# Feed-forwards of a hybrid encoder trunk as seven block products instead of eight, with the weight sums on GpSimd

## The chip, the cores and the metric

The kernel runs on one core of a Trainium2 chip. The core's engines work side by side, each with its own queue of instructions: TensorE (PE in the rows; its weight loads are PEld), VectorE (DVE), ScalarE (ACT), GpSimd (POOL), and SyncE (SP), which here only starts transfers. The metric is the device time of one execution in microseconds (us).

## What is computed

Two layers over 512 tokens of 1024 features, all in float32. Each layer has two SwiGLU feed-forwards with 2816 inner features, so there are four feed-forwards in a run; between them stand a mixer (layer 0: sliding-window attention beside a gated recurrence; layer 1: a gated delta rule), layer normalisations and a gated embedding. Cut to what matters here:

```
def swiglu(x, wg, wu, wd):
    return (jax.nn.silu(x @ wg) * (x @ wu)) @ wd

for i in range(2):
    x = layer_norm(DN_ALPHA * x + 0.5 * swiglu(x, ffn1_wg[i], ffn1_wu[i], ffn1_wd[i]), ...)
    y = mixer_ab(x, ...) if i % 2 == 0 else mixer_c(x, ...)
    x = layer_norm(DN_ALPHA * x + y, ...)
    x = layer_norm(DN_ALPHA * x + 0.5 * swiglu(x, ffn2_wg[i], ffn2_wu[i], ffn2_wd[i]), ...)
    x = x + sigmoid(x @ ple_wg[i] + ple_bg[i]) * (p[i] @ ple_wp[i])
```

## The kernel before

Activations lie with features on the 128 partitions and the 512 tokens along the free axis, so x is eight tiles `xf[k]` of 128x512, and the inner features of a feed-forward are 22 tiles `hs[j]`. Weights come as tiles of 128x128, packed by the host in the order of use: one transfer on SyncE's queue brings eight of them (512 KB, tile name `wr`), into one of three buffers.

A float32 product is carried by three float32r matmuls (`mm3`). Both operands are cut into a rounded part `hi` and the remainder `lo = src - hi`: ScalarE makes `hi` (the rows' CAST), VectorE subtracts (TENSOR_TENSOR with two inputs). The weights are cut four tiles at a time, 128x512 per instruction, by the generator `splitter`, which runs some steps (`self.ahead`; a step is one product of a block in the changed kernel, where `AHEADS` sets it) in front of the products; activations are cut by `split` when they are made.

`ffn` makes the gate and up products of two inner tiles at a time (`group`: four PSUM banks advance together over the eight k), and `evac` turns them into `hs[j]` with a Silu on ScalarE and a product on VectorE. Then `resid_ln` makes the down products, one output tile of 22 k at a time (`mtile`), adds them to the residual and takes sums for the layer normalisation; the two adds of sums per output tile are the only large work of GpSimd (`add.l.tensor_tensor` with `G`). The last output tile is made by halves of the tokens, so that `tail` and `apply` normalise the first half under the products of the second.

Tile by tile that is 3 x 8 x 22 = 528 weight tiles for a feed-forward, 1584 matmuls, of 512 columns except for those of the last output tile (and of the first group, where a layer normalisation stands in front of it), which go by 256.

The order of issue is made at build time. The main stream is TensorE's; everything else is a generator that yields operations, and `tick` lets each go on as far as its operands are there by a rough clock of every engine (`Eng.cost`). Each engine then works through its own queue in that fixed order. Nearly every instruction is issued from one line, `getattr(self.e, op.name)(*op.a, **op.kw)` in `Eng.issue`, which is L100 in the rows of before (L151 in the order of the changed kernel); so rows are told apart by tile names: `wr` raw weights, `t` any 128x512 tile of the pool, `ps` a PSUM bank.

Of the kernel before, what the change touches and what calls it, by code (L numbers as in the profile page):

```python
# [35 lines left out]
NRAW = 3  # L36
NTILES = 4 * 3 * KD * MF + 2 * (KD + 2) * KD + (14 + 8) * KD + 8 + (32 + 8) * KD
NUNITS = -(-NTILES // NSLOT)
# [4 lines left out]
# columns of the packed per-partition vectors  # L43
# [14 lines left out]
# columns of the constant table: identity, ones, cumulative-sum triangle, causal mask,  # L58
# compact identity, masks of the block-doubling levels
# [16 lines left out]
def cells(ap):  # L76
    """the 128-element columns of its tile that an access touches"""
    name = ap.tensor.name
    dims = list(ap.ap)
    c0 = ap.offset % dims[0][0]  # L80
    c1 = c0 + sum((n - 1) * st for st, n in dims[1:])
    return [(name, c) for c in range(c0 // P, c1 // P + 1)]


class Eng:
    """Issues to an engine and keeps a rough clock of it, by which the order of issue of
    independent work is chosen. eng.f(...) issues, eng.l.f(...) makes an Op to be issued later."""
# [25 lines left out]
    def at(self, op):  # L113
        """when the operands are there"""
        ready = self.k.ready
        return max([ready.get(c, 0.0) for x in op.ins for c in cells(x)] + [0.0])

    def cost(self, op):
# [7 lines left out]
        if self.kind == "PE":  # L126
            if op.name == "transpose":
                return max(0.027, 0.000417 * w)
            if ins[0].dtype == F32R:
                return max(0.107, 0.000417 * w) + 0.0025  # L130
            return 2 * max(0.107 * n / P, 0.000417 * w) + 0.004
# [18 lines left out]
        return 0.04 + (0.0008 if op.name == "memset" else 0.0023) * n  # L150
# [10 lines left out]
class Kern:  # L161
    def __init__(self, tc, a, order):
# [5 lines left out]
        self.nslot = 0  # L168
        self.units, self.raw = {}, {}
        self.ndma = self.nsplit = 0  # L170
# [62 lines left out]
    def tick(self, share=None):  # L233
        """share: the time that chains may take on the tensor engine now"""
# [39 lines left out]
    def until(self, cond):  # L274
        """hold the main stream until the chains have issued what it needs"""
# [8 lines left out]
    def settle(self, *aps):  # L284
        """chains go on while the main stream's next operands are not there"""
# [7 lines left out]
    def dma_unit(self, v):  # L293
        t = self.wraw.tile([P, NSLOT * P], F32, tag="wraw", name=self.name("wr"))
        self.nc.sync.dma_start(t, self.a["w"][v])
        self.raw[v] = t
        self.landing(t, 3.5)

    def splitter(self):
        """splits the weights some half units ahead of their use"""  # L300
        while self.nsplit < 2 * NUNITS:
            v = self.nsplit
            while v > self.nslot // HSLOT + self.ahead:
                yield None
            while self.ndma <= min(v // 2 + NRAW - 1, NUNITS - 1):
                self.dma_unit(self.ndma)
                self.ndma += 1
            r = self.raw[v // 2] if v % 2 == 0 else self.raw.pop(v // 2)
            r = r[:, (v % 2) * HSLOT * P:(v % 2 + 1) * HSLOT * P]
            hi, lo = self.tl(), self.tl()  # L310
            for c0, c1 in FIRST if v == 0 else ((0, HSLOT),):
                if c1 <= HSLOT:
                    c = slice(c0 * P, c1 * P)
                    yield self.S.l.copy(hi[:, c].bitcast(F32R), r[:, c])
                    yield self.V.l.tensor_tensor(lo[:, c].bitcast(F32R), r[:, c], hi[:, c], ALU.subtract)
                    self.units[v] = (hi, lo)
            self.nsplit += 1

    def w(self, desc):
        """the next weight tile of the stream, as its two parts"""  # L320
        u, s = divmod(self.nslot, HSLOT)
        if s == 0:
            # the splitter goes first when it is late
            late = self.nsplit <= u + 2
            prio = 0 if late else 4
            if prio != self.split_gen[2] and self.split_gen in self.gens:
                self.gens.remove(self.split_gen)
                self.split_gen[2] = prio
                self.enlist(self.split_gen)
            self.until(lambda: u in self.units)  # L330
            self.units.pop(u - 1, None)
        self.order.append(desc)
        self.nslot += 1
        hi, lo = self.units[u]
        s = slice(s * P, (s + 1) * P)
# [19 lines left out]
    def split(self, src, eng=None):  # L355
        """hi = rounded src, lo = src - hi; src in SBUF or PSUM"""
# [8 lines left out]
    def group(self, descs, x, nk=KD, halves=False):  # L365
        """the m tiles of a group advance together over k; with halves, tokens 0-255 first"""
# [20 lines left out]
    def x(self, k, cs):  # L387
        """layer input k, once its normalisation is issued"""
# [12 lines left out]
    def ffn(self, i, n, l):  # L401
        wg, wu, wd = f"ffn{n}_wg", f"ffn{n}_wu", f"ffn{n}_wd"
        self.hs = [None] * MF
        self.ahead = 4

        def evac(j, pg, pu):
            t = self.tl()
            yield self.S.l.activation(t, pg, AF.Silu)
            self.psfree(self.S)
            yield self.V.l.tensor_tensor(t, t, pu, ALU.mult)  # L410
            self.psfree(self.V)
            self.hs[j] = yield from self.split(t)

        for g in range(MF // 2):
            descs = []
            for j in (2 * g, 2 * g + 1):
                descs.append(lambda k, j=j: (wg, i, k, j))
                descs.append(lambda k, j=j: (wu, i, k, j))
            ps = self.group(descs, self.x, halves=g == 0 and n == 2)
            for j in range(2):  # L420
                self.spawn(evac(2 * g + j, ps[2 * j], ps[2 * j + 1]), 1)
        self.resid_ln(i, l, 0.5, lambda m: (lambda k: (wd, i, k, m)), self.h, MF, 0, 1)

    def resid_ln(self, i, l, fac, desc, y, nk, ngroup, nhalf):
        """x = LN(alpha x + fac y); y comes as 8 PSUM tiles: the first ngroup advance together
        over k, the last nhalf are made by halves of the tokens, so that the normalisation of the
        first half runs under the products of the second. Sums are taken about the mean of the
        first 128 features."""
        S, V, G, PE = self.S, self.V, self.G, self.PE
        self.__dict__.pop("x", None)  # L430
        xf = self.xf
# [39 lines left out]
        for m in range(max(ngroup, 1), KD - nhalf):  # L471
            if m == KD - nhalf - 2 or nk == KD:
                self.ahead = AHEADF if nk == MF else AHEADO
# [80 lines left out]
    def ple_p(self, i, ms):  # L554
        """products of p, made where the main stream would wait for a normalisation"""
# [13 lines left out]
    def ple(self, i):  # L569
# [26 lines left out]
        if last:  # L596
            # the last one by halves of the tokens, each on its way out under the other
# [17 lines left out]
        self.x = x  # L615

    def softplus(self, x, n):
        """max(x,0) + log1p(exp(-|x|)), log1p by 2 atanh(e/(2+e))"""
# [74 lines left out]
    def attn(self, j, hh, q):  # L693
        """one head, two pairs of 128-query blocks; keys of the block and of the one before"""
# [59 lines left out]
    def conv(self, p_, cols, bias=None):  # L754
        """causal depthwise convolution over the free axis, taps w[0..3] per partition"""
# [142 lines left out]
    def gdn(self, h):  # L898
# [9 lines left out]
        # decay: dt[j, i] = exp(gc_i - gc_j), j <= i  # L908
# [3 lines left out]
        # token-major k, q (for the norms) and v  # L912
# [37 lines left out]
        # U = (I + N)^-1, 32x32 diagonal blocks first (compact), then 64 and 128  # L950
# [15 lines left out]
        # level s: with the 2s blocks [lo | hi], the product of U11 N12 with U22 makes U12; two  # L966
        # chunks share a pass, the hi (then the lo) columns of both being 32
# [52 lines left out]
        # scan over the blocks  # L1020
# [48 lines left out]
    def run(self):  # L1069
# [3 lines left out]
        with ExitStack() as es:  # L1073
# [12 lines left out]
            r0 = self.wraw.tile([P, NSLOT * P], F32, tag="wraw", name="wr0")  # L1086
            self.raw[0] = r0
            self.ndma = 1
# [209 lines left out]
```

## Time and profile before

| | us |
|---|---|
| three runs | 2113.21, 2113.46 (median), 2114.86 |
| span of the profiled execution | 2113.2 |
| PE busy | 2093.3 (99%) |
| DVE busy | 1102.8 (52%) |
| ACT busy | 867.1 (41%) |
| POOL busy | 145.5 (7%) |

The profiled execution has no time of its own beside its span; the span lies 0.3 us under the median. Times below are in us from the span's start. A duration in a row runs from an instruction's start to its end and holds its waits once it has been dispatched; instructions of one engine overlap a little, so the pace of a run of equal ones is the length of the run, less the overhang of the last, by their number.

### The profile page before, as it was taken

The page shows a single profiled execution, that of the slowest core. Times are in us where ns is not written, and L with a number is a line of the kernel's source. Part 1 is how long each engine was busy: PE and PEld are TensorE (multiplying, and loading weights), DVE is VectorE, ACT ScalarE, POOL GpSimd, SP SyncE. Part 2 cuts the span into 40 slices and gives each one's busy share as a digit, 9 for nine tenths or more (in the row PEclk, how much of TensorE's full clock was granted, in tenths as well). Part 3 has the DMA queues.
Part 4 walks back from the last instruction along what each step waited for, and adds up shares of the span by engine and source line. Part 5 has one row for each costly group of instructions (what it writes and reads, how often), then busy time and mean ns, then how long its engine had stood idle before and what let it go on. Part 6 is the DMA issues. An engine that isn't in the chain of part 4 may idle for free. (4 is left out here: it accounts for less than half of the span.)

```text
span 2113.2 us, 29415 instructions
## 1 busy us (share of the span) xinstructions
PE 2093.3 (99%) x11773; PEld 1757.3 (83%) x11773; DVE 1102.8 (52%) x2146; ACT 867.1 (41%) x1795; POOL 145.5 (7%) x120
## 2 busy tenths in 40 slices
PE   9999999999999999999999999999999999999999
PEld 7888888878888888898888888977777898888888
DVE  5334345778833334484333344867776763343456
ACT  4323224665623322263323223674754452232244
POOL 0000012001100001100000011020210200000110
PEclk9999999999999999999999999999999999999999
DMA  5323234113232323313232324132221213232331
GB/s 180 118 81 105 85 110 150 41 52 99 79 102 81 119 80 101 133 56 110 90 109 80 110 87 143 33 85 65 51 63 59 90 62 119 80 113 78 108 120 51
DMA packets 55754, 194.38 MB, mean 92 GB/s; under 512 B 6320, under 2 KB 7232, under 8 KB 55616
## 3 DMA queue, kind: packets, MB, share of 16 engines
q1 hardware_dynamic: 54432, 188.81, 27.6%
q0 software_dynamic: 1184, 3.69, 0.9%
q8 instruction: 92, 1.51, 0.3%
q14 instruction: 46, 0.38, 0.1%
HBM read 190.35 MB, written 2.11 MB: 91 GB/s over the span
## 5 line engine op out<-in xcount | busy, mean ns | idle before, releaser
L100 PE MATMUL ps<-t,t 128*128 128x512 f32 (+5 forms) x10640 | 2049.8, 354 | 7.1 <-ACT t L100 4.3
L100 PEld LDWEIGHTS ps<-t,t 128*128 128x128 f32 (+3 forms) x10640 | 1692.4, 184 | 319.2 <-issue 17.8
L100 DVE TENSOR_TENSOR t<-wr,t 128x512 fp32r<-128x512 f32 (+1 forms) x695 | 485.7, 741 | 163.7 <-ACT t L100 159.3
L100 ACT CAST t<-wr 128x512 fp32r<-128x512 f32 (+1 forms) x695 | 393.8, 616 | 193.2 <-DMA wr<-w 192.9
L100 DVE TENSOR_TENSOR t<-t,ps 128x512 f32<-128x512 f32 (+1 forms) x126 | 71.1, 565 | 440.3 <-PE ps L100 251.9
L100 ACT ACTIVATE t<-ps 128x512 f32<-128x512 f32 (+2 forms) x172 | 78.9, 462 | 501.6 <-PE ps L100 501.3
L100 DVE TENSOR_TENSOR t<-t,t 128x512 fp32r<-128x512 f32 (+3 forms) x314 | 176.0, 571 | 62.6 <-ACT t L100 56.1
L100 POOL TENSOR_TENSOR t<-t,t 128x512 f32<-128x512 f32 x64 | 98.3, 1555 | 1601.8 <-DVE t L100 1581.9
L100 ACT CAST t<-t 128x512 fp32r<-128x512 f32 (+1 forms) x253 | 130.0, 518 | 162.7 <-DVE t L100 160.0
L100 ACT ACTIVATE t<-t 128x512 f32<-128x512 f32 (+1 forms) x118 | 66.4, 572 | 260.6 <-DVE t L100 256.6
L100 DVE SCALAR_TENSOR_TENSOR t<-ps,t 128x512 f32<-128x512 f32 (+2 forms) x74 | 43.9, 600 | 212.5 <-PE ps L100 212.5
L100 DVE SCALAR_TENSOR_TENSOR t<-ps,vec,t 128x511 f32<-128x511 f32 (+3 forms) x92 | 68.2, 743 | 21.1 <-ACT t L100 17.4
L100 ACT ACTIVATE t<-t,vec,der 128x256 f32<-128x256 f32 x96 | 55.2, 597 | 5.8 <-DVE t L100 5.8
L100 ACT ACT_TABLE_LOAD x37 | 47.5, 1283 | 10.7 <-DVE t L100 9.5
L100 DVE SCALAR_TENSOR_TENSOR t<-t,t 128x512 f32<-128x512 f32 (+2 forms) x64 | 38.2, 605 | 21.0 <-ACT t L100 19.7
L100 DVE SCALAR_TENSOR_TENSOR t<-t,der,t 128x256 f32<-128x256 f32 x96 | 45.8, 477 | 0.0
L100 ACT COPY t<-ps 128x512 f32<-128x512 f32 (+1 forms) x59 | 33.0, 567 | 28.1 <-PE ps L100 27.9
L100 PEld LDWEIGHTS ps<-cst,t 128*128 128x128 f32 (+1 forms) x300 | 35.4, 148 | 10.8 <-issue 2.3
L100 PE MATMUL ps<-cst,t 128*128 128x128 f32 (+2 forms) x300 | 41.5, 261 | 1.4 <-DVE t L100 1.4
L100 DVE TENSOR_TENSOR t<-t 128x256 f32<-128x256 f32 x96 | 40.1, 420 | 2.6
L100 POOL TENSOR_TENSOR y<-y,sm 128x8 f32<-128x8 f32 (+1 forms) x16 | 22.9, 1434 | 190.0 <-DVE y L100 189.9
L100 ACT ACTIVATE t<-ps,vec 128x512 f32<-128x512 f32 x28 | 19.4, 699 | 23.8 <-PE ps L100 23.8
(66 smaller groups left out, 412.8 us busy)
## 6 DMA issues: line engine op xcount, KB each, us to landing
wr<-w SPq DMA_DIRECT2D x346, 512.0 KB, 4.2
t<-x SPq DMA_DIRECT2D x8, 256.0 KB, 6.3
t<-p SPq DMA_DIRECT2D x8, 256.0 KB, 5.0
t<-gcd POOLq DMA_DIRECT2D x8, 256.0 KB, 5.3
out<-t SPq DMA_DIRECT2D x7, 256.0 KB, 2.0
t<-bias POOLq DMA_DIRECT2D x8, 192.0 KB, 3.7
cst<-cst SPq DMA_DIRECT2D x1, 352.0 KB, 5.8
wr<-w SPq DMA_DIRECT2D x2, 128.0 KB, 2.9
```

Source lines behind the costliest of these rows:

```text
L100: getattr(self.e, op.name)(*op.a, **op.kw)
```

## The change

In most of a feed-forward two k tiles, two output tiles and the two halves of the tokens now form a 2x2 by 2x2 block product, made by seven products of 256 columns instead of eight (the scheme of Winograd). `block` makes one such block over `n` pairs of k tiles: seven products (`PRODUCTS`), each 3n matmuls of 256 columns; three of them go into the PSUM bank R one after the other, and between them ScalarE takes a copy of R (`snap`), for which the next product into R waits. The five sums that the seven weight forms need are made of raw weights by `adder` on GpSimd (four instructions a block); the seven forms are then cut into hi and lo by `splitter`. The forms of the activations (four differences and seven or eight splits for a pair of tiles, all of 256 columns) are made by `xforms` for x and by `hforms` for the inner features. `gate_up(j)` is a block whose two output tiles are gate and up of inner tile j; `down(mp, ...)` one whose output tiles are 2mp and 2mp+1.

The 22 inner tiles are taken in three parts of 6, 8 and 8; after each part its share of the down products is added to the residual. Two of the inner tiles (`NPLAIN`), and the last two output tiles in the third part, are still made by plain products. Per feed-forward there are 20 blocks of `gate_up` with 4 pairs, 4 of `down` with 3 pairs, and 4 + 3 of `down` with 4 pairs. Raw buffers go from 3 to 5, pool tiles from 93 to 89; the rough clock has new costs for matmuls and GpSimd. Mixers and embeddings keep their code.

The diff, cut to its core:

```diff
-NRAW = 3
+NRAW = 5
+PARTS = (6, 8, 8)
+NPLAIN = 2
+PRODUCTS = ("a11", "a12", "s2", "s3", "s1", "a22", "s4")
+AHEADS, SUMAHEAD = 4, 3
...
+    def adder(self):
+        G = self.G.l
+        for it, (v, u, n) in enumerate(self.st.items):
...
+            a11, a12, a21, a22 = r0[:, 0:n], r0[:, n:2 * n], r1[:, 0:n], r1[:, n:2 * n]
+            s1, s2, s3, s4 = (self.tl() for _ in range(4))
...
+            yield G.tensor_tensor(s1[:, 0:n], a21, a22, ALU.add)
...
+            yield G.tensor_tensor(s2[:, 0:n], s1[:, 0:n], a11, ALU.subtract)
...
+            yield G.tensor_tensor(s3[:, 0:n], a11, a21, ALU.subtract)
...
+            yield G.tensor_tensor(s4[:, 0:n], a12, s2[:, 0:n], ALU.subtract)
...
+    def block(self, descs, forms, pairs, done):
...
+        def snap(name, p_):
+            yield S.activation(snaps[name], p_[:, TA], AF.Copy, scale=scale)
...
+        product(R, "a11", True, True)
+        self.spawn(snap("s1", R), 0)
+        X = self.ps()
+        product(X, "a12", True, True)
+        self.spawn(done("c11", X, snaps["s1"], lambda: "s1" in have), 1)
+        wait("s1")
+        product(R, "s2", False, True)
+        self.spawn(snap("s2", R), 0)
+        Q = self.ps()
+        product(Q, "s3", True, True)
+        self.spawn(snap("q1", Q), 0)
+        wait("s2")
+        product(R, "s1", False, True)
+        self.spawn(snap("s4", R), 0)
+        wait("q1")
+        product(Q, "a22", False, True)
+        self.spawn(done("c21", Q, snaps["s2"], lambda: True), 1)
+        self.spawn(done("c22", snaps["q1"], snaps["s4"], lambda: "s4" in have), 1)
+        wait("s4")
+        product(R, "s4", False, True)
+        self.spawn(done("c12", R, None, lambda: True), 1)
...
+    def diffs(self, b0, b1, F, key, home=None, free=None):
...
+            yield V.tensor_tensor(d, x, y, ALU.subtract)
...
+            yield from self.halves_split(d, hi, lo)
...
+        def gate_up(j):
...
+                if name == "c11":
+                    yield V.tensor_tensor(g[:, cs], p_[:, TA], s, ALU.add)
+                    self.psfree(self.V)
+                    yield S.activation(g[:, cs], g[:, cs], AF.Silu)
+                elif name == "c12":
+                    yield S.activation(g[:, cs], p_[:, TA], AF.Silu)
+                    self.psfree(self.S)
+                elif name == "c21":
+                    yield V.tensor_tensor(u[:, cs], p_[:, TA], s, ALU.add)
+                    self.psfree(self.V)
+                else:
+                    yield G.tensor_tensor(u[:, cs], p_, s, ALU.add)
...
+                if n[half] == 2:
+                    yield V.tensor_tensor(h[:, cs], g[:, cs], u[:, cs], ALU.mult)
...
+        def down(mp, pairs, end):
...
+                if s is not None:
+                    yield V.tensor_tensor(x, x, s, ALU.add)
+                if name == "c22":
+                    yield V.tensor_tensor(x, x, p_, ALU.add)
+                else:
+                    yield V.scalar_tensor_tensor(x, p_[:, TA], 0.5, x, ALU.mult, ALU.add)
```

How the queues move is seen at two places. First VectorE in the middle of the first feed-forward's gate and up products. Before, weights are cut one after the other, and now and then an inner tile (`t_660`, `t_667`) is made and cut:

```order
L100 TENSOR_TENSOR t_632<-wr_545,t_631 128x512
L100 TENSOR_TENSOR t_650<-wr_579,t_649 128x512
L100 TENSOR_TENSOR t_660<-t_660,ps_502 128x512
L100 TENSOR_TENSOR t_664<-t_660,t_663 128x512
L100 TENSOR_TENSOR t_667<-t_667,ps_504 128x512
L100 TENSOR_TENSOR t_672<-t_667,t_671 128x512
L100 TENSOR_TENSOR t_684<-wr_579,t_683 128x512
L100 TENSOR_TENSOR t_702<-wr_613,t_701 128x512
```

In the changed program, at one block of `gate_up` (its c11 and c21 read the banks `ps_2355` and `ps_2394`; `t_2434` and `t_2452` are cut from sums, the 256-wide rows are products and forms of inner tiles):

```order
L151 TENSOR_TENSOR t_2325<-ps_2355,t_2327 128x256
L151 TENSOR_TENSOR t_2379<-t_2169,t_2378 128x512
L151 TENSOR_TENSOR t_2398<-wr_2058,t_2397 128x512
L151 TENSOR_TENSOR t_2415<-wr_2058,t_2414 128x512
L151 TENSOR_TENSOR t_2434<-t_2332,t_2433 128x512
L151 TENSOR_TENSOR t_2326<-ps_2394,t_2327 128x256
L151 TENSOR_TENSOR t_2325<-t_2325,t_2326 128x256
L151 TENSOR_TENSOR t_2452<-t_2333,t_2451 128x512
L151 TENSOR_TENSOR t_2457<-t_2325,t_2456 128x256
L151 TENSOR_TENSOR t_2325<-t_2325,t_2326 128x256
L151 TENSOR_TENSOR t_2485<-t_2160 128x256
L151 TENSOR_TENSOR t_2492<-t_2331,t_2491 128x512
```

What moved: cuts of weight forms now come seven to a block, and small instructions with two tile inputs stand between them. Second, GpSimd, which before has nothing in its queue between the start and the adds of the first layer normalisation:

```order
L100 MEMSET sm 128x8
L100 ISA
L100 TENSOR_TENSOR t_2023<-t_80,t_81 128x512
L100 TENSOR_TENSOR t_2022<-t_2022,t_2112 128x512
L100 TENSOR_TENSOR t_2023<-t_2023,t_82 128x512
```

In the changed program the same queue, in the gate and up products of the first feed-forward, holds the four sums of each block (inputs `wr`), and after the sums of the next block the c22 of an earlier one (`t_1558`):

```order
L151 TENSOR_TENSOR t_1455<-wr_1286 128x512
L151 TENSOR_TENSOR t_1456<-t_1455,wr_1241 128x512
L151 TENSOR_TENSOR t_1457<-wr_1241,wr_1286 128x512
L151 TENSOR_TENSOR t_1458<-wr_1241,t_1456 128x512
L151 TENSOR_TENSOR t_1578<-wr_1405 128x512
L151 TENSOR_TENSOR t_1579<-t_1578,wr_1358 128x512
L151 TENSOR_TENSOR t_1580<-wr_1358,wr_1405 128x512
L151 TENSOR_TENSOR t_1581<-wr_1358,t_1579 128x512
L151 TENSOR_TENSOR t_1558<-t_1560 128x256
```

What moved: GpSimd goes from two adds per output tile at the end of a feed-forward to work in every block, all of it with inputs in SBUF.

## Rows read from the trace of the kernel before

**Rows 1.** Page: busy time of the engines and waits of all TensorE matmuls.
```profile
PE 2093.3 (99%) x11773; PEld 1757.3 (83%) x11773; DVE 1102.8 (52%) x2146; ACT 867.1 (41%) x1795; POOL 145.5 (7%) x120
L100 PE MATMUL ps<-t,t 128*128 128x512 f32 (+5 forms) x10640 | 2049.8, 354 | 7.1 <-ACT t L100 4.3
```

**Rows 2.** Windows inside the four feed-forwards: busy us, instructions, granted clock, DMA share, GB/s.
```profile
core 0: us, PE busy (x) PEld busy (x) DVE busy (x) ACT busy (x) POOL busy (x), PEclk, DMA share, GB/s
20.00:340.00 320.00, 320.00 (x1413) 264.97 (x1412) 127.39 (x212) 100.24 (x181) 15.12 (x10) 1.00 0.32 104
...
570.00:880.00 310.00, 310.00 (x1387) 257.42 (x1387) 118.70 (x179) 94.98 (x170) 12.30 (x8) 1.00 0.31 100
960.00:1290.00 330.00, 330.00 (x1457) 273.27 (x1456) 125.90 (x191) 100.81 (x180) 12.30 (x8) 1.00 0.31 101
...
1720.00:2040.00 320.00, 320.00 (x1414) 264.96 (x1413) 121.68 (x182) 96.14 (x173) 15.31 (x10) 1.00 0.33 105
```

**Rows 3.** Timeline, PE: unbroken runs of 512 and of 256 columns (start, length).
```profile
149.81 113.95 PE L100 MATMUL ps<-t,t 128*128 128x512 f32 x502
...
923.74 16.48 PE L100 MATMUL ps<-t,t 128*128 128x256 f32 x136
```

**Rows 4.** Timeline, DVE and ACT: runs of equal instructions, back to back, GpSimd idle.
```profile
30.57 3.09 DVE L100 TENSOR_TENSOR t<-wr,t 128x512 fp32r<-128x512 f32 x5
...
368.99 1.42 DVE L100 TENSOR_TENSOR t<-t,t 128x256 f32<-128x256 f32 x4
...
248.04 2.71 ACT L100 CAST t<-wr 128x512 fp32r<-128x512 f32 x5
```

**Rows 5.** Timeline, DVE and POOL, around 324: layer normalisation adds beside weight cuts.
```profile
322.23 3.31 POOL L100 TENSOR_TENSOR t<-t,t 128x512 f32<-128x512 f32 x2 [11.95 <-DVE t L100]
...
322.00 5.89 DVE L100 TENSOR_TENSOR t<-wr,t 128x512 fp32r<-128x512 f32 x6
...
323.80 1.74 POOL L100 TENSOR_TENSOR t<-t,t 128x512 f32<-128x512 f32 x1
324.31 1.77 DVE L100 TENSOR_TENSOR t<-wr,t 128x512 fp32r<-128x512 f32 x1
```

**Rows 6.** Timeline, the same two engines around 527: a 256-column DVE instruction.
```profile
525.94 1.75 POOL L100 TENSOR_TENSOR t<-t,t 128x512 f32<-128x512 f32 x1
526.45 1.52 DVE L100 TENSOR_TENSOR t<-t,t 128x256 f32<-128x256 f32 x1
```

**Rows 7.** Timeline around 523: POOL beside DVE instructions with one PSUM input.
```profile
521.72 2.55 POOL L100 TENSOR_TENSOR t<-t,t 128x512 f32<-128x512 f32 x2 [155.99 <-DVE t L100]
522.67 0.67 DVE L100 SCALAR_TENSOR_TENSOR t<-ps,t 128x512 f32<-128x512 f32 x1
...
528.49 0.41 DVE L100 SCALAR_TENSOR_TENSOR t<-ps,t 128x256 f32<-128x256 f32 x1
528.83 1.18 DVE L100 TENSOR_TENSOR t<-t,t 128x256 f32<-128x256 f32 x1
```

**Rows 8.** Groups, by form: scaling of x on DVE, and evacuations on ACT.
```profile
L100 DVE TENSOR_SCALAR t<-t 128x512 f32<-128x512 f32 x14 | 5.9, 418 | 0.3 <-ACT t L100 0.2
L100 ACT ACTIVATE t<-ps 128x256 f32<-128x256 f32 x12 | 4.5, 377 | 3.5 <-PE ps L100 3.5
```

**Rows 9.** Page: issues of the weight transfers (count, KB each, us to landing).
```profile
wr<-w SPq DMA_DIRECT2D x346, 512.0 KB, 4.2
```

More of the change, by code (lines that the diff above doesn't have):

```diff
@@ L312, in splitter @@
                 if c1 <= HSLOT:
[L313 to L317, printed above, removed]
-    def w(self, desc):
[L321 to L332, printed above, removed]
+                    c = slice(c0 * P, min(c1 * P, n))
@@ L402, in ffn, with xforms @@
         wg, wu, wd = f"ffn{n}_wg", f"ffn{n}_wu", f"ffn{n}_wd"
-        self.hs = [None] * MF
+        S, V, G = self.S.l, self.V.l, self.G.l
         self.ahead = 4
+        xdone, xs, xf = self.xdone, self.xs, self.xf
+        XF = {}
+        last = len(PARTS) - 1
+        hf, HF, HP = {}, {}, {}
+        scaled = []
+        def xforms(kp):
+            k0, k1 = 2 * kp, 2 * kp + 1
+            while not (xdone(k0) and xdone(k1)):
+                yield None
+            for which, k, cs in (("a11", k0, TA), ("a12", k1, TA), ("s4", k1, TB)):
+                XF[kp, which] = tuple(t[:, cs] for t in xs(k))
+            yield from self.diffs(xf[k0], xf[k1], XF, kp, tuple(t[:, TB] for t in xs(k0)),
+                                  lambda: self.nplain == NPLAIN)
+            for m in (k0, k1):
+                yield V.tensor_scalar(xf[m], xf[m], ALPHA, None, ALU.mult)
+            scaled.append(kp)
@@ L406, in evac @@
         def evac(j, pg, pu):
             t = self.tl()
-            yield self.S.l.activation(t, pg, AF.Silu)
+            yield S.activation(t, pg, AF.Silu)
             self.psfree(self.S)
-            yield self.V.l.tensor_tensor(t, t, pu, ALU.mult)
+            yield V.tensor_tensor(t, t, pu, ALU.mult)
             self.psfree(self.V)
[L412 to L421, printed above, removed]
@@ new lines, in down, with done @@
+        def down(mp, pairs, end):
+            ends = {}
+            def done(name, p_, s, ready):
+                m, cs = 2 * mp + int(name[1]) - 1, TA if name[2] == "1" else TB
+                x = xf[m][:, cs]
+                while not ready() or len(scaled) < KD // 2:
+                    yield None
+                if s is not None:
+                    yield V.tensor_tensor(x, x, s, ALU.add)
+                if name == "c22":
+                    yield V.tensor_tensor(x, x, p_, ALU.add)
+                else:
+                    yield V.scalar_tensor_tensor(x, p_[:, TA], 0.5, x, ALU.mult, ALU.add)
+                    self.psfree(self.V)
+                ends[m] = ends.get(m, 0) + 1
+                if ends[m] == 2:
+                    end(m)
+            self.snapscale = 0.5
+            self.block((lambda k: (wd, i, k, 2 * mp), lambda k: (wd, i, k, 2 * mp + 1)),
+                       lambda kp, r: HF.get((kp, r)), pairs, done)
+            self.snapscale = 1.0
@@ new lines, in ffn @@
+        self.nplain = 0
+        for kp in range(KD // 2):
+            self.spawn(xforms(kp), 2.5)
+        descs = []
+        for j in range(NPLAIN):
+            descs.append(lambda k, j=j: (wg, i, k, j))
+            descs.append(lambda k, j=j: (wu, i, k, j))
+        ps = self.group(descs, self.x, halves=n == 2)
+        for j in range(NPLAIN):
+            self.spawn(evac(j, ps[2 * j], ps[2 * j + 1]), 1)
+        self.nplain = NPLAIN
+        j1 = 0
+        for n_, part in enumerate(PARTS):
+            j0, j1 = j1, j1 + part
+            self.ahead = AHEADS
+            for j in range(j0, j1):
+                if j % 2 == 0:
+                    self.spawn(hforms(j // 2, n_ == last), 1.2)
+                if j >= NPLAIN:
+                    gate_up(j)
+            pairs = range(j0 // 2, j1 // 2)
+            if n_ < last:
+                for mp in range(KD // 2):
+                    down(mp, pairs, lambda m: None)
@@ L471, in resid_ln @@
         for m in range(max(ngroup, 1), KD - nhalf):
-            if m == KD - nhalf - 2 or nk == KD:
-                self.ahead = AHEADF if nk == MF else AHEADO
+            self.ahead = AHEADO
             self.spawn(take(m, self.mtile(desc(m), y, nk), FULL, True, G), 1)
@@ L615, in ple @@
         self.x = x
+        self.xdone = self.xs = lambda k: new[k]
     def softplus(self, x, n):
```

326 lines of the change are left out of this document (290 added, 36 removed).

## Prediction

> **What bounds the kernel now.** I read the page first, then windows inside the four feed-forwards, then single stretches of the timeline. The page says that TensorE is busy for 2093.3 of the 2113.2 us, and that its 10640 main matmuls were preceded by 7.1 us of idle time in all [rows 1]. In four windows that lie inside the feed-forwards it never pauses, at the full granted clock (1.00, the 2.4 GHz level), while VectorE is busy 38 to 40%, ScalarE 31% and GpSimd 4 to 5% [rows 2]. So the count and the pace of matmuls set the time there, and everything else has room.
>
> The pace: 502 matmuls of 512 columns took 113.95 us, 0.227 us each; 136 of 256 columns took 16.48, of which some 0.16 is the last one's overhang, so 0.120 each [rows 3]. Half the columns cost 53%, not 50%: each matmul carries about 13 ns that do not shrink.
>
> **TensorE's share of the change.** A feed-forward before has 528 tiles x 3 = 1584 matmuls; without the last output tile that is 1518 of 512 columns (344.6 us) and 132 of 256 (15.8): 360.4 us. After: the blocks hold 20x4 + 4x3 + 7x4 = 120 pairs, each 7 x 3 matmuls of 256 columns, 2520 in all; the plain rest is 32 tiles of gate and up (96 of 512 columns) and 16 of down by halves (96 of 256). That is 21.8 + 2616 x 0.120 = 335.7 us. Four feed-forwards save 4 x 24.7 = 99 us; a pace of 0.121 for the narrow ones would make it 89. The first group that goes by halves is the same in both.
>
> The Trainium skill ("TensorE: Matmul & The Clock Gate", Back-to-back issue gap) gives 518 cycles for 512 columns and 262 for 256, a fixed cost of some 2.5 ns. By it 5688 fewer wide and 9936 more narrow ones would save 142 us, by the rows 99; the rows decide.
>
> **What VectorE and GpSimd must do instead.** The question is whether they can feed TensorE at that pace. Alone, VectorE cuts 512 columns every 0.602 us (five in 3.09, less 0.08 overhang) and does a 256-column instruction with two tile inputs every 0.335 (four in 1.42) [rows 4]. But when GpSimd works, the two take turns. Six cuts took 5.89 us with two GpSimd adds among them, instead of 6 x 0.602 + 0.08 = 3.69: 1.10 us lost per add [rows 5]. In detail: the add ends at 325.54, the cut dispatched at 324.31 ends at 326.08, 0.54 later, its whole working time behind the add [rows 5]; a 256-column one ends at 527.97, 0.28 behind the add that ended at 527.69 [rows 6]. An instruction with one input in PSUM is not held: two adds in 2.55 us while such ones went by at 0.67 [rows 7]. So each GpSimd sum of 512 columns stops the VectorE instructions with two SBUF inputs for about 1.1 us. The changed kernel has four such sums per block, and nearly all that it adds on VectorE has two SBUF inputs.
>
> The Trainium skill says this as a rule ("SBUF — State Buffer", Who interferes with whom): the pair of ports is locked for whole instructions, and VectorE instructions with two SBUF inputs contend with GpSimd ones that read SBUF. The rows agree (1.10 us of loss against none), and the rule speaks against this change: it says that the sums are not free on an idle engine.
>
> Now the stages, for one feed-forward, as VectorE's own line of time:
> - *Two blocks of gate_up* (two inner tiles): 14 cuts (8.43), 15 instructions of 256 columns with two SBUF inputs (4 products of gate and up, 11 for the forms of the pair; 5.03), 4 adds from PSUM (0.34 by the step from 528.49 to 528.83 [rows 7], 1.36): 14.8. GpSimd: 8 sums x 1.10 and two c22 of 256 columns, which no row shows. I bound these by half and the whole of 1.10 and take half, being half the columns: 9.9. Together 24.7; the four adds from PSUM can lie under GpSimd work, so 23.4 to 24.7, and I take 24.2. TensorE needs 168 x 0.120 = 20.2; before it was 96 x 0.227 = 21.8. So +2.4, times ten: **+24**, bounds +16 and +29.
> - *A down block of four pairs*: 7 cuts (4.21), 4 adds with two SBUF inputs (1.34), 3 with PSUM (1.02), 4 sums (4.4): 11.0, less at most 1.02; TensorE 10.1; before 10.9. I take 10.5. Four in the second part: **-1.6** (-3.3 to +0.4).
> - *A down block of three pairs*: cuts and sums of 384 columns at three quarters (no row; between half and whole): 3.2 + 1.3 + 1.0 + 3.3 = 8.8, less at most 1.0; TensorE 7.6; before 8.2. I take 8.5. Four: **+1.3** (-0.8 to +2.6).
> - *Start*: 32 forms of x (10.7), 8 scalings (3.4 at 0.42 [rows 8]), 12 cuts (7.2), 4 sums (4.4), some evacuation (1.9): 27.6 beside 21.8 of plain products. Only the third product of the first block needs differences, so I take **+2** (0 to +5.8).
> - *Last part's down* (three blocks, then 16 plain tiles): TensorE 30.2 + 11.5 = 41.7, before 43.9. VectorE 3 x 6.6 + 5.7 for the mean, GpSimd 12 sums and 10 adds of the normalisation x 1.10: 49.7 if nothing overlaps. I take 44.5: **+0.6** (-2.2 to +5.8).
>
> Sum: +26 us per feed-forward (+10 to +44), 4 x 26 = +105. The mixers and embeddings keep their instructions, so nothing is put down for them. ScalarE stays below: a pair of gate_up blocks has 14 casts at 0.52 [rows 4] and some 20 instructions of 256 columns, 0.38 each by the nearest row [rows 8], 15 of 24 us. Transfers are as many bytes as before at about 100 GB/s [rows 2], 4.2 us to landing [rows 9], with five buffers instead of three. The planner's lead of four products (some 5.8 us) covers a single late cut; it can't cover a pace that stays too slow.
>
> The profiled execution spans 2113.2 us, within 0.3 of the median: 2113 + 105 = **2218 us**, 5% slower. TensorE would then idle for some 105 + 99 = 200 us.
>
> **Rivals.**
> 1. *The turns don't add up and TensorE stays the bound.* Then the 99 us come out: 2014, with 0 to 25 for waits on the snapshots, 2014 to 2040. For it: VectorE's own work is only 14.8 of 20.2 us per gate_up pair, and the pair of engines now shares little time [rows 2]. Against it: it needs a loss below 0.6 us per GpSimd instruction (5.4 us for nine equal ones), and the rows show 1.10 [rows 5]. Chance 0.13.
> 2. *Equal.* The stages even out: VectorE runs ahead in down blocks, all PSUM work hides, and the gate_up pairs come to 22 us. Against it: even the sum of lower bounds is +10 per feed-forward (2153), and the lead is four products. 2100 to 2130, chance 0.05.
> 3. *The lateness chains.* ScalarE's queue is in order: a cast that waits for a late GpSimd sum stands in front of a snapshot, and TensorE waits for that before the next product into R. Each block has three such waits, with one product of 1.44 us to hide a snapshot of 0.38 [rows 8]. If one wait in two costs 0.5 us, 124 blocks x 0.75 add 93: 2310, and up to 2400 at every wait. It decides where GpSimd falls a whole block behind. For it: all four sums of a block are needed by the third to seventh product; against it: the adder may lead by up to seven products. Chance 0.10.
>
> The forecast has the rest, 0.72, within 2130 to 2310.
>
> **How the numbers follow.** The lower bounds give 2153 and the upper 2290; I let the range reach from 2120, where the bounds of the unshown widths and a somewhat smaller loss still end, to 2340 with half of rival 3. Outside lie rival 1, a part of rival 2, and the far end of rival 3: 0.2. A measurement of this kernel can tell about 0.2% from no change, 4 us. Faster holds rival 1 and a third of rival 2: 0.14; same 0.03; slower 0.83.
>
> **What would show it.** Right: VectorE busy (with its waits) above 75% in the feed-forwards, GpSimd near 45 to 60% with a mean of 1.4 to 1.75 us per 512-column sum, cuts of 512 columns with a mean above 1 us, TensorE waiting mostly for VectorE tiles, some 200 us of it, within gate_up blocks, and dense stretches at 0.120 between. Wrong: cuts that stay near 0.7 us beside busy GpSimd, TensorE above 95%, or idle time that ScalarE or GpSimd ends rather than VectorE; and a narrow pace other than 0.120 when weights change with every matmul. A clock below 1.00 in the feed-forwards would be a cost that I have not counted.

## The result, and the profile after

The changed kernel takes **2524.85 us** (median of four runs, 2519.36 to 2529.83), the kernel before 2114.05 in runs beside it: a ratio of **1.194**, 95% interval 1.192 to 1.196. It is slower, as forecast, but by 411 us and not by 105: 185 us above the upper end of the range.

The page of the changed kernel: busy time, granted clock in forty slices, the chain that ended last by engine, and the matmuls.

```profile
PE 2183.4 (86%) x16021; PEld 2015.0 (80%) x16021; DVE 2147.5 (85%) x3648; ACT 1316.5 (52%) x3067; POOL 933.2 (37%) x688
...
PEclk8999988999989999899899988999999989999889
...
DVE 42%; PE 42%; issue 7%; ACT 7%; DMA 1%; POOL 1%; SPq 0%; DVEq 0%; ACTq 0%; POOLq 0%
...
L151 PE MATMUL ps<-t,t 128*128 128x256 f32 (+5 forms) x14888 | 2138.7, 306 | 323.9 <-ACT t L151 238.6
```

Before, the main matmuls waited 7.1 us in all [rows 1]; now it is 323.9, mostly for ScalarE. VectorE's busy time has nearly doubled. Of the chain that ended last, 42% lies on VectorE and 42% on TensorE. Windows inside the feed-forwards, to be read against [rows 2], show TensorE at 82 to 84% and its clock at 0.90 to 0.92:

```profile
core 0: us, PE busy (x) PEld busy (x) DVE busy (x) ACT busy (x) POOL busy (x), PEclk, DMA share, GB/s
20.00:460.00 440.00, 364.88 (x2612) 350.32 (x2610) 387.94 (x578) 216.53 (x502) 211.18 (x153) 0.90 0.24 78
...
960.00:1400.00 440.00, 370.26 (x2604) 352.70 (x2605) 389.99 (x602) 229.54 (x525) 183.29 (x133) 0.92 0.25 79
```

The groups by form say what VectorE does there. Alone, a cut of 512 columns came every 0.602 us and a two-input instruction of 256 columns every 0.335 [rows 4]; a row's duration is some 0.08 us more than such a pace. The mean durations are now 0.81 to 0.95 us and 0.72 (in run 1 below 0.72 to 0.74 and 0.44):

```profile
L151 DVE TENSOR_TENSOR t<-t,t 128x512 fp32r<-128x512 f32 x478 | 450.2, 945 | 68.6 <-ACT t L151 66.3
L151 DVE TENSOR_TENSOR t<-wr,t 128x512 fp32r<-128x512 f32 x535 | 425.7, 809 | 108.8 <-ACT t L151 103.1 <-PE ps L151 1.3
L151 DVE TENSOR_TENSOR t<-t,t 128x256 f32<-128x256 f32 x572 | 409.7, 719 | 10.4 <-POOL t L151 4.5 <-ACT t L151 0.4
...
L151 POOL TENSOR_TENSOR t<-t,wr 128x512 f32<-128x512 f32 x108 | 152.7, 1414 | 10.0 <-DVE t L151 1.7
...
L151 POOL TENSOR_TENSOR t<-t 128x256 f32<-128x256 f32 x80 | 62.0, 775 | 691.6 <-ACT t L151 678.3 <-DVE y L151 13.3
```

Two pairs of gate_up blocks in the third part of the first feed-forward, and a stretch right behind a wait of TensorE's, as windows:

```profile
301.71:332.41 30.70, 24.82 (x170) 24.41 (x169) 24.08 (x35) 14.40 (x34) 13.80 (x11) 0.83 0.22 68
332.41:363.16 30.75, 24.82 (x170) 24.41 (x169) 24.09 (x35) 14.39 (x34) 13.79 (x11) 0.83 0.20 69
338.20:341.00 2.80, 2.78 (x13) 2.78 (x14) 1.81 (x4) 1.41 (x3) 0.00 (x0) 0.50 0.20 53
```

VectorE is busy 24.1 us per pair, where the prediction's sum was 24.2; but the pair takes 30.7 us. TensorE needs 24.8 us instead of 20.2, because its granted clock is 0.83 in the mean, and 0.50 (the 1.2 GHz level) right after a wait. The timeline inside the second pair shows how a block goes:

```profile
331.85 6.54 DVE L151 TENSOR_TENSOR t<-t,t 128x256 f32<-128x256 f32 x6
...
332.71 1.36 POOL L151 TENSOR_TENSOR t<-t,wr 128x512 f32<-128x512 f32 x1
...
334.03 1.73 POOL L151 TENSOR_TENSOR t<-wr,wr 128x512 f32<-128x512 f32 x1
335.73 1.44 POOL L151 TENSOR_TENSOR t<-wr,t 128x512 f32<-128x512 f32 x1
337.48 0.41 ACT L151 CAST t<-t 128x256 fp32r<-128x256 f32 x1 [3.33 <-DVE t L151]
337.79 0.38 ACT L151 ACTIVATE t<-ps 128x256 f32<-128x256 f32 x1
...
338.22 0.58 PE L151 MATMUL ps<-t,t 128*128 128x256 f32 x1 [2.77 <-ACT t L151]
```

GpSimd does its sums back to back, VectorE's instructions come through between them (six of them take 6.54 us), and a 256-column form that VectorE makes is late. ScalarE's cast of that form waits 3.33 us at the head of its in-order queue; the snapshot behind it (ACTIVATE out of `ps`) starts at 337.79, and TensorE, which may not write R before, starts again at 338.22. So the row that names ScalarE as the releaser shows a messenger. The start of the next burst, on GpSimd alone:

```profile
345.96 0.74 POOL L151 TENSOR_TENSOR t<-t 128x256 f32<-128x256 f32 x1 [8.80 <-ACT t L151]
346.66 1.74 POOL L151 TENSOR_TENSOR t<-wr 128x512 f32<-128x512 f32 x1
```

c22 (one of a block's four results, added up from two snapshots) waits 8.80 us for these, which wait for products at a slow clock, and the four sums stand behind it in GpSimd's queue.

### The profile page after: what moved, and what is told of

Its sections match the earlier page's. It is cut to its first block, busy times and chain, and to the rows that moved or that the text cites. A ratio compares the mean times of both kernels' runs of the same rounds, so it can differ in the third digit from the quotient of the medians.

```text
span 2528.1 us, 42421 instructions
## 1 busy us (share of the span) xinstructions
PE 2183.4 (86%) x16021; PEld 2015.0 (80%) x16021; DVE 2147.5 (85%) x3648; ACT 1316.5 (52%) x3067; POOL 933.2 (37%) x688
## 4 chain that ended last, share of the span: by engine, by line
DVE 42%; PE 42%; issue 7%; ACT 7%; DMA 1%; POOL 1%; SPq 0%; DVEq 0%; ACTq 0%; POOLq 0%
DVE t L151 42%; PE ps L151 42%; ACT t L151 7%; POOL t L151 1%; DMA wr<-w 0%; DVE y L151 0%; DMA t<-p 0%; ACT L151 0%; DMA t<-x 0%; DMA t<-gcd 0%; SPq L1479 0%; POOL y L151 0%; DVEq L151 0%; DMA gcd<-t 0%; ACTq L151 0%
## 5 line engine op out<-in xcount | busy, mean ns | idle before, releaser
L151 PE MATMUL ps<-t,t 128*128 128x256 f32 (+5 forms) x14888 | 2138.7, 306 | 323.9 <-ACT t L151 238.6
L151 PEld LDWEIGHTS ps<-t,t 128*128 128x128 f32 (+2 forms) x14888 | 1949.4, 199 | 467.0 <-ACT t L151 277.5
L151 DVE TENSOR_TENSOR t<-t,t 128x256 f32<-128x256 f32 (+4 forms) x1642 | 1182.3, 758 | 102.3 <-ACT t L151 86.5
L151 ACT CAST t<-t 128x512 fp32r<-128x512 f32 (+2 forms) x1049 | 504.6, 508 | 512.0 <-DVE t L151 504.0
L151 DVE TENSOR_TENSOR t<-wr,t 128x512 fp32r<-128x512 f32 (+2 forms) x589 | 473.3, 817 | 112.3 <-ACT t L151 106.0
L151 ACT ACTIVATE t<-ps 128x256 f32<-128x256 f32 (+2 forms) x668 | 249.8, 376 | 334.6 <-PE ps L151 333.4
L151 ACT CAST t<-wr 128x512 fp32r<-128x512 f32 (+2 forms) x589 | 346.8, 603 | 6.5 <-DMA wr<-w 5.9
L151 POOL TENSOR_TENSOR t<-wr 128x512 f32<-128x512 f32 (+1 forms) x124 | 200.2, 1615 | 201.0 <-DMA wr<-w 98.1
L151 POOL TENSOR_TENSOR t<-wr,wr 128x512 f32<-128x512 f32 (+1 forms) x124 | 203.6, 1642 | 7.8 <-DVE t L151 7.8
L151 POOL TENSOR_TENSOR t<-wr,t 128x512 f32<-128x512 f32 (+1 forms) x124 | 179.5, 1447 | 4.6 <-DVE t L151 4.6
```

## The experiments

Each is compared with the kernel before on the same chip (medians 2114.2 to 2115.5 us). Single times are single runs, those with a range had several.

**1. No reading on GpSimd beside VectorE.** Each sum (four in each of 124 blocks, 496 in all; "five" in the section on the change is a slip) becomes two memsets, so that the sums are left out and constants stand in their place.

```diff
-            yield G.tensor_tensor(s1[:, 0:n], a21, a22, ALU.add)
+            for _ in range(2):
+                yield G.memset(s1[:, 0:n], 0.01)
```

> Each of the four weight sums of a block is replaced by two GpSimd memsets of the same tile (about 1.05 us by the 0.526 us row of a memset of 512 columns): GpSimd stays as busy and in the same order, but no longer reads SBUF. The sums are thereby left out: constants stand in the products. Theory (VectorE and GpSimd take turns whenever both read SBUF, and the turns make VectorE late): VectorE needs about 16 us per two gate and up blocks and TensorE 20.2, so TensorE is the bound again: 2010 to 2080 us, cuts of 512 columns near 0.69 us. Rival (the order of the queues alone, with GpSimd held by c22 and ScalarE held by late casts, makes the stalls, whatever GpSimd reads): the order is kept, so 2350 us or more.

Measured: 2127.09. The page's busy times, and then windows of the first block with what is ahead of it, of eight gate_up blocks, of a pair of them in the third part, and of the last part's end:

```profile
PE 2037.5 (96%) x16021; PEld 1904.7 (90%) x16021; DVE 1697.9 (80%) x3648; ACT 1324.1 (62%) x3067; POOL 675.7 (32%) x1184
```

```profile
4.18:46.34 42.16, 36.71 (x180) 31.02 (x181) 36.76 (x88) 28.74 (x60) 10.70 (x20) 0.94 0.52 192
109.27:189.91 80.64, 80.64 (x675) 80.64 (x674) 62.02 (x126) 53.34 (x125) 35.20 (x67) 1.00 0.32 110
271.01:291.17 20.16, 20.16 (x171) 20.16 (x170) 16.47 (x35) 14.40 (x35) 9.50 (x19) 1.00 0.31 107
332.35:367.55 35.20, 24.63 (x186) 23.70 (x184) 33.40 (x55) 19.48 (x41) 16.96 (x17) 0.93 0.57 194
```

That is 398 us less than the changed kernel. VectorE's busy time falls by 450 us, 0.91 for each of the 496 sums. Eight blocks run at 10.08 us each without a pause, at full clock. GpSimd's share there is about as before (35.2 of 80.6 us, 44%), but apart from c22 it only writes. Its work per block is shorter, though, 4.4 us instead of 6.9, and a memset waits for no weights, so the run takes away a little more than the reading; that the loss is VectorE's shows in its own mean durations, given above. The Trainium skill ("SBUF — State Buffer", Who interferes with whom) says that VectorE instructions with two SBUF inputs contend with GpSimd instructions that read SBUF and not with those that only write it; this run agrees (450 us). But the time is still 12 us above the kernel before and outside the expectation: at the edges TensorE works 24.63 of 35.20 us.

**2. The sums on VectorE.**

```diff
-        G = self.G.l
+        G = self.V.l
```

> The four weight sums of a block are made by VectorE instead of GpSimd; only c22 stays on GpSimd. Theory (a sum on GpSimd costs VectorE 1.10 us of waiting, on VectorE itself 0.60): VectorE needs 14.8 + 8 x 0.60 + 2 x 0.4 = 20.4 us per two gate and up blocks, TensorE 20.2, a down block of four pairs 9.0 against 10.1; 2050 to 2200 us. Rival (VectorE has too much to do and GpSimd relieves it): VectorE gains 540 instructions, 0.6 us each over the run is some 270 us on the engine that is already 85% busy: 2600 us or more.

Measured: 2251.71 (2250.07 to 2252.24), ratio 1.064 (1.063 to 1.066). The page, and then a pair of gate_up blocks as a window:

```profile
PE 2078.9 (92%) x16021; PEld 1937.0 (86%) x16021; DVE 1982.9 (88%) x4144; ACT 1319.4 (59%) x3067; POOL 213.4 (9%) x192
```

```profile
264.91:285.07 20.16, 20.16 (x170) 20.16 (x169) 19.16 (x37) 13.17 (x32) 1.55 (x2) 1.00 0.29 100
```

273 us better than on GpSimd, with a pair at TensorE's own 20.16. The 496 sums cost VectorE 285 us against run 1, 0.57 each: less than the 0.91 that they cost it when GpSimd made them. The time is 52 us above what the theory allowed; the steady pairs are where it put them, the first block (20.0 us) and the first down block of each part (15.8 to 16.9) are not.

**3. c22 on VectorE**, so that the sums no longer stand behind it.

```diff
-                    yield G.tensor_tensor(u[:, cs], p_, s, ALU.add)
+                    yield V.tensor_tensor(u[:, cs], p_, s, ALU.add)
```

> Only c22 of gate_up moves from GpSimd to VectorE, so that GpSimd's queue no longer waits for the end of a block and the sums can start when their weights land. VectorE's load per pair of blocks stays about the same (24). Theory (the sums come as one burst at the end of a block because they stand behind c22, and in that burst VectorE's forms and ScalarE's snapshots behind them come late): the sums spread, 2250 to 2350 us. Rival (the total of the turns is what counts): 2480 to 2530 us.

Measured: 2435.64, between the ranges of the theory and the rival: 89 us less, and VectorE stays 88% busy.

**4. A planner that knows of the turns.** The rough clock books one common resource for two-input instructions of both engines (and takes a GpSimd instruction as 0.0023 us a column, not 0.0028).

```diff
+            t = self.k.port(t, 0.03 + (0.00104 if self.kind == "V" else 0.0022) * n)
```

> The rough clock that orders the queues is told of the turns: VectorE instructions with two SBUF inputs and GpSimd sums book a common port, 0.03 us + 0.00104 or 0.0022 us per column. Same instructions in another order. Theory (part of the time above the sum of VectorE's work is lost because ScalarE's queue puts casts that come late in front of snapshots): with the lateness known the order changes, 2300 to 2420 us, not below 2200, where VectorE's work alone would stand. Rival (order does nothing, load is all): 2500 us or more.

Measured: 2489.84, 35 us less, outside both ranges. Some pairs fell to 21.4 us, but the first down products of two parts took 29.8 and 36.7: another order moves the lateness.

**5 and 6. More plain tiles at the start** (`NPLAIN` 4 in groups of two), with run 1's memsets (the sums are constants) and with run 2's sums on VectorE.

```diff
-NPLAIN = 2
+NPLAIN = 4
```

> The kernel with memsets in place of the sums (sums left out, constants in the products), and four plain inner tiles at the start of a feed-forward instead of two. In the run with memsets every steady block took TensorE's own 10.08 us, yet the first feed-forward took 363.4 us, as before the change. Theory (the rest went at the edges: 6.9 us at the first block, where the forms of x are late, some more behind each part and at the layer normalisation): 1.6 us more of plain products each, 5 to 7 us less waiting: 2095 to 2115 us. Rival (the wait at the start only moves to another place): 2127 to 2140.

> Sums on VectorE, and four plain inner tiles at the start. Theory (VectorE is about as long as TensorE in the blocks, and lateness shows where it has forms to make besides: at the start some 20 us of the first feed-forward): 10 to 15 us less in each, 2190 to 2215 us. Rival (VectorE's total sets the time, wherever it waits): 2240 to 2260.

Measured: 2137.49 and 2237.60. Both theories missed; the rival of run 5 was right, and run 6 lies 2 us below its rival's range. The first block of run 5 as a window:

```profile
51.55:70.61 19.06, 13.56 (x85) 12.47 (x84) 18.05 (x45) 11.31 (x31) 4.13 (x9) 0.76 0.12 42
```

It takes 19.06 us instead of 10.08, with VectorE busy for 18.05. More cover doesn't remove the wait, it moves along; in run 7 below, which makes no forms of the inner features, the block behind the same four plain tiles takes 10.07.

**7. Blocks for gate and up alone**, sums on VectorE: down is by tiles as before, in two parts, no forms of the inner features are made, and the tiles of x are no longer scaled one by one.

```diff
-PARTS = (6, 8, 8)
+PARTS = (10, 12)
...
-NPLAIN = 2
+NPLAIN = 4
...
+            self.resid_ln(i, l, 0.5, off, y, part, 0, 1)
```

> One half of the change alone, with the sums on VectorE: seven products for gate and up (18 blocks, four plain inner tiles), the down products plain as before in two parts of 10 and 12 inner tiles; so no forms of the inner features, no snapshots in the down products. TensorE: 18 x 10.08 + 240 x 3 x 0.227 = 344.9 us against 360.4. VectorE in two blocks: 14 cuts and 8 sums x 0.60, 4 adds, 4 products, 2 cuts of inner tiles: 17.1 of 20.2 us. Theory: VectorE has room, so TensorE bounds: 2113 - 4 x 15.5 = 2051, with edges 2050 to 2100: faster than both. Rival (the block form itself, its snapshots and starts, costs more than it gives): 2113 or more.

Measured: **2093.22** (2089.92 to 2095.53), ratio 0.990 (0.988 to 0.992): 1% below the kernel before, and the fastest of all. Five blocks in a window:

```profile
206.76:257.16 50.40, 50.40 (x422) 50.40 (x421) 46.15 (x81) 31.65 (x70) 3.71 (x5) 1.00 0.33 105
```

VectorE needs 9.23 us of each block's 10.08.

**8. The same with the sums on GpSimd** (`G = self.G.l` in the adder).

> The same half of the change with the sums on GpSimd. VectorE in two blocks: 14 cuts (8.4), 4 adds (1.4), 4 products (1.3), 2 cuts (1.2), and 8 sums x 1.10 and two c22 of waiting (9.9): 22.2 of 20.2 us. Theory (turns): above the run with the sums on VectorE by 2 us per pair of blocks and more through late snapshots and the clock: 2120 to 2250 us. Rival (GpSimd relieves VectorE where VectorE has room): equal to that run or less.

Measured: 2207.98 (2206.96 to 2210.27), ratio 1.044 (1.042 to 1.046): the engine of the sums alone makes 115 us. Six blocks as a window, and then GpSimd's timeline at the start of one:

```profile
208.76:281.02 72.26, 62.74 (x506) 61.05 (x505) 63.32 (x73) 37.35 (x84) 41.41 (x31) 1.00 0.29 88
```

```profile
242.64 0.74 POOL L150 TENSOR_TENSOR t<-t 128x256 f32<-128x256 f32 x1 [5.05 <-ACT t L150]
```

A block takes 12.04 us with VectorE busy for 10.55: c22, which waits 5.05 us, seems to hold the sums here too; run 9 tests it.

**9. Run 8 with c22 on VectorE** (run 3's edit).

> The kernel with blocks for gate and up only and sums on GpSimd, with c22 moved to VectorE. There a pair of blocks took 24.1 us with VectorE busy for 21.1, so neither VectorE nor TensorE (20.9) filled it. Theory (GpSimd's queue is the loop: c22 waits for the end of a block, the four sums, 6.2 us, stand behind it, and the next cuts behind those): without c22 in front the sums start as the weights land, and the period falls to VectorE's work, 8.4 + 1.4 + 2.0 + 1.2 + 8 x 1.10 = 21.8 us: some 2.2 us less for each of 36 pairs, 2120 to 2150 us. Rival (the period is made by the turns themselves): 2190 to 2215 us.

Measured: 2147.44, as the theory had it. Five blocks:

```profile
223.63:278.00 54.37, 52.92 (x422) 50.90 (x421) 53.28 (x66) 31.12 (x70) 32.75 (x20) 1.00 0.31 98
```

10.87 us a block, 21.7 a pair, VectorE 98% busy. With nothing else in GpSimd's queue the prediction's way of adding, with these blocks' counts, holds to 0.1 us (21.8) in this stretch; the first four blocks of the run took 12.6 to 15.2. Of the 115 us between runs 7 and 8, by this run c22's place in the queue makes 61, and 54 stay with the sums on GpSimd alone.

**10. The casts of the forms on VectorE**, so that they don't stand ahead of snapshots.

```diff
-        yield self.S.l.copy(hi.bitcast(F32R), src)
+        yield self.V.l.tensor_copy(hi.bitcast(F32R), src)
```

> The changed kernel with the rounding casts of all 256-column forms (differences and halves of inner tiles) on VectorE instead of ScalarE, about 0.2 us each there by half of the 0.418 us row for 512 columns. VectorE gets some 2.2 us more in a pair of gate and up blocks. Theory (a late form holds ScalarE's queue, and the snapshots behind it hold TensorE): ScalarE no longer waits for forms, TensorE's waits on ScalarE (248 us) mostly go, and the time falls in spite of the load: 2380 to 2490 us. Rival (VectorE's load alone sets the time): 36 to 45 pairs' worth of 2.2 us more, 2600 us or above.

Measured: 2579.6, slower still, between the two ranges. TensorE's waits, to be read against the changed kernel's 248.3 us for ScalarE and 90.6 for VectorE:

```profile
PE ps L151 <- DVE t L151: 342.0, 208, 8.7
PE ps L151 <- ACT t L151: 53.4, 35, 5.3
```

The message now comes from VectorE itself, and the waits together are longer: most of the lateness that ScalarE's queue handed on was VectorE's. As VectorE has 110 us more to do here, the run doesn't exclude that the queue adds a share.

**11. Run 7 with two plain tiles** (`NPLAIN` 2 again).

> The fastest kernel so far (blocks for gate and up, sums on VectorE) with two plain inner tiles instead of four, so 20 blocks in a feed-forward. Each pair of blocks saves 1.6 us of products: 4 x 1.6 = 7 us, 2084 to 2090, if the forms of x are ready after 21.8 us of plain products. Rival: the first block waits for them, VectorE having some 10.7 us of forms, 7 of cuts and 2.4 of sums to do in that time beside the tail of the normalisation, and 2 to 8 us are lost in each feed-forward: 2092 to 2115.

Measured: 2115.22 (2113.09 to 2117.6), ratio 1.000 (0.999 to 1.001). 22 us are lost, as the rival had it at its upper end: here, unlike in runs 5 and 6, the first block had wanted more cover (13.76 us instead of 10.07 in the first feed-forward).

**12. The sums a block earlier**: on GpSimd each block's four sums stand ahead of the c22 that they stood behind.

```diff
-AHEADS, SUMAHEAD = 4, 3
+AHEADS, SUMAHEAD = 4, 7
```

> The changed kernel with SUMAHEAD 7 instead of 3: the adder may lead the cuts by a whole block, so that on GpSimd's queue the four sums of a block stand ahead of the c22 of the block before it instead of behind it; instructions and their numbers stay. Theory (each block's period is set by GpSimd's burst of four sums that waits for c22, not by VectorE's sum alone): a pair of gate_up blocks in a third part falls from 30.7 us towards VectorE's 24.2, TensorE's clock there rises to 0.95 and more, the time falls by 150 to 250 us, to 2280 to 2380. Rival A (VectorE's late forms hold the loop wherever the sums stand): 2480 to 2540, pairs of 29 and more. Rival B (the sums, now earlier, hold VectorE's port while the forms of the same block are due, so that the wait only moves): 2400 to 2480, with snapshots still held behind late casts.

Measured: 2483.55 (2469.14 to 2485.99), ratio 1.172 (1.168 to 1.176); the theory missed by 104 us, and the time lies in rival A's range, though some pairs are below its 29 us. The page, and a pair of gate_up blocks in the third part:

```profile
PE 2157.7 (87%) x16021; PEld 1992.8 (80%) x16021; DVE 2178.6 (88%) x3648; ACT 1317.4 (53%) x3067; POOL 939.9 (38%) x688
```

```profile
329.52:357.68 28.16, 22.42 (x170) 21.90 (x169) 24.69 (x34) 13.93 (x34) 13.45 (x10) 0.94 0.19 66
```

That pair takes 28.2 us where the changed kernel's took 30.7, and the eight blocks of that part take 108.5 instead of 118.0; it doesn't come near VectorE's 24.2. VectorE's busy time over the run, 2147.5 us before this edit, is not less but 31 us more. So the burst behind c22 is one cause, worth 41 us by this run and 89 by run 3 (which also takes c22 off GpSimd), and most of the excess stays without it.

## Why the prediction was too low

**What held.** The direction, and the mechanism: the sums on GpSimd stop VectorE. Run 1 shows it by taking it away (398 us), runs 7 and 8 by the engine of the sums alone (115 us). The loss per sum, 1.10 us forecast, measured 0.91 over all. That VectorE's 24.1 us per pair came out so near to 24.2 is partly luck: against run 1's pair (16.47) the eight sums cost 7.6 us and not 8.8, and the rest, c22's share with it, was longer than forecast. The pace of 0.120 us for a narrow matmul held too (80.64 us for eight blocks of 84). Two of the named signs failed: the cuts' mean stayed below 1 us (0.81 to 0.95), and TensorE's waits name ScalarE (248.3 us) and not VectorE (90.6), which the prediction had listed under "wrong"; the timeline shows why the name misleads.

**The step that failed** is the sum of the stages: VectorE's own line of time was taken for the period of each stage, with the planner's lead of four products, which "covers a single late cut", to make it so. It went wrong by size in three ways. The stages of the first feed-forward as windows: start and first block; three gate_up blocks, the four down blocks; eight gate_up, four down; eight gate_up; and the last part's down products with the normalisation.

```profile
4.28:59.11 54.83, 40.85 (x180) 33.27 (x181) 49.00 (x88) 28.77 (x60) 18.40 (x13) 0.86 0.40 147
59.11:95.88 36.77, 32.03 (x253) 31.25 (x253) 32.54 (x66) 19.66 (x48) 14.36 (x13) 0.97 0.25 77
95.88:138.63 42.75, 35.91 (x254) 33.87 (x252) 40.33 (x62) 20.86 (x52) 24.47 (x19) 0.88 0.25 81
138.63:241.78 103.15, 88.19 (x673) 85.92 (x674) 90.94 (x128) 51.91 (x124) 52.16 (x38) 0.95 0.26 87
241.78:291.63 49.85, 44.70 (x338) 42.50 (x337) 48.24 (x63) 23.38 (x52) 29.67 (x20) 0.97 0.23 77
291.63:409.65 118.02, 97.50 (x674) 96.07 (x673) 90.84 (x131) 54.58 (x128) 50.50 (x37) 0.84 0.23 76
409.65:474.81 65.16, 49.27 (x357) 47.56 (x355) 61.61 (x95) 33.95 (x73) 29.92 (x26) 0.89 0.38 130
```

- *The gate_up pair*, +2.4 us forecast, measured 30.7 - 21.8 = +8.9 in the third part. VectorE's 24.1 us are there, but 6.6 us of idle time as well: block after block the sums wait for c22, c22 for snapshots, the snapshots for casts and products, and VectorE's forms for the sums. That is a loop, and a lead doesn't cover a lateness that comes back in every block. The nineteen gate_up blocks after the first took 257.9 us in the first feed-forward; I had 230. VectorE is busy for 214 of them, less than forecast: the whole excess is waiting.
- *The edges.* Start and first block took 54.8 us (35.9 forecast), the eight down blocks of the first two parts 92.6 (76), the last part with the normalisation 65.2 (44.5). I had costed them as VectorE's sums too, with part of it hidden. Here VectorE's own line was too short: it is busy for 199 us of these stages, against the 156 that I had. Together the first feed-forward takes 470.5 us, against the 386 of these terms; VectorE is busy for 413.5 of it, 27 more than that, and the other 57 are its idle time.
- *The clock*, named as a cost not counted. The forecast left TensorE 2093.3 - 99 = 1994 us of busy time; it has 2183.4, 189 more, while its idle time is 344.7 us instead of 224, 121 more: together the 310 us by which the profiled execution missed. Run 1 does the same 16021 matmuls in 2037.5, so 146 of the 189 go with the lower clock; the other 43 are in run 1 too, whose mean granted clock is 0.983. These are not apart from the waits: where the waits go, the clock is back at 1.00 (run 1, run 2's pair).

Two slips in the working carry no weight: the saving that stands beside the 99 us comes to 143 and not 142, and the lower bound of the three-pair blocks is -1.5 and not -0.8.

**Rivals.** The third, the chain through ScalarE's queue, gave 2310 to 2400 and is the nearest in form: in the timeline a snapshot does stand behind a cast that waits. But the late operand there is VectorE's form and not a sum of GpSimd's, and run 10, without these casts in the queue, is no faster. The first, TensorE stays the bound, needed a loss below 0.6 us per GpSimd instruction; it was 0.91. Even with no loss at all (run 1) the 99 us didn't come out: 2127 and not 2014. What the steady blocks gain, the edges take: in run 1's first feed-forward, start and first block take 42.2 us for some 31.9 of matmuls at full pace, and the last part's end 35.2 for 24.6, with VectorE busy for 36.8 and 33.4 of them. Run 7, which makes no forms of the inner features and has four plain tiles ahead, keeps 22 us of gain.

**What stays open.** How the excess over the forecast divides between the burst, VectorE's longer line at the edges and the clock is accounted for above, but not separated by a run for each in the changed kernel (runs 7 to 9 part the burst from the turns in theirs). Whether ScalarE's queue adds a share of its own is open. c22 on VectorE together with the earlier sums or the planner's booking was not tried.

## What to carry to other kernels

Work given to an idle engine may not be free: here, where both engines read SBUF, a sum on GpSimd cost VectorE 0.91 us and on VectorE itself 0.57, so price such a move by the busy engine's loss, from a row where both run. A sum of busy times is a lower bound of a stage's period; here it became the period only where nothing in the in-order queues beside it waited for the stage's own result (run 9: 21.7 against 21.8; the changed kernel: 30.7 against 24.2). Use the cheaper algorithm where its extra operands are few (gate and up, 1% gained), not where every product needs new ones.

## What the hardware showed that was not expected

TensorE's clock falls after waits that are short. In the changed kernel, TensorE's timeline in the third part shows a wait of some 3 us in each block of 15.4 us:

```profile
338.22 13.00 PE L151 MATMUL ps<-t,t 128*128 128x256 f32 x84 [2.77 <-ACT t L151]
354.38 11.82 PE L151 MATMUL ps<-t,t 128*128 128x256 f32 x84 [3.15 <-ACT t L151]
```

84 narrow matmuls take 13.00 us behind the wait of 2.77, 11.82 behind that of 3.15, and 10.08 at the full clock (run 1); right behind the first the clock is 0.50 (window 338.20:341.00 above), in the mean of the pair 0.83. In run 8 the wait is half as long, in each block of 12.04 us, and the window above has the clock at 1.00:

```profile
213.38 10.45 PE L150 MATMUL ps<-t,t 128*128 128x256 f32 x84 [1.59 <-ACT t L150]
```

The Trainium skill ("TensorE: Matmul & The Clock Gate", Part 1: The HAM clock gate) has the clock follow how busy the array has been; the rows agree (1.00 with waits of 1.59 us, 0.50 behind one of 2.77). A pair's two waits, 5.9 us, bring 4.7 us more of matmul time with them. The length of a single wait doesn't tell its price: the shorter one costs more here (2.9 us against 1.7), and in run 12 a block behind a still longer one took no more than 11.86:

```profile
323.62 11.86 PE L151 MATMUL ps<-t,t 128*128 128x256 f32 x84 [4.09 <-ACT t L151]
```
